# Four sums of a weight quad in another order, and in other tiles

## Chip, core and metric

The kernel runs on one core of a Trainium2 chip. The metric is the time of one execution on the device in microseconds (us); lower is better.

## What is computed

One layer of a hybrid decoder on a sequence of 2048 rows of 1024 values, with 16 learned meta rows ahead of it, all in fp32:

```python
hn = rms_norm(h, norm_g)
proj = jnp.einsum('bld,de->ble', hn, w_in)              # 1024 -> 8 x 512
cx, cb, cc, cg, q, k, v, rg = jnp.split(proj, N_PROJ, axis=-1)
conv_out = short_conv_branch(cx, cb, cc, conv_w) * jax.nn.silu(cg)
qf, kf = rotary(q) * d**-0.5, rotary(k)                 # 4 heads of 128
ret = head_group_norm(retention_chunkwise(qf, kf, v), ret_norm_g)
mixed = jnp.concatenate([conv_out, ret * jax.nn.silu(rg)], axis=-1)
h = h + jnp.einsum('ble,ed->bld', mixed, w_out)
out = rms_norm(h, final_g)[:, N_META:]
```

## The kernel before

The work is two projections, in and out, and between them a short convolution and a chunked retention. TensorE multiplies fp32 values that are split into two parts: a high part, which ScalarE rounds (`wh` for weights, `mh` for the other operand, line 119 or 122), and a low part, the value minus the high part, which VectorE subtracts (`wl`, `ml`, line 120 or 123). A product is then three matmuls for each step of 128: low by high, high by low, high by high.

Most of the projections run as quads: 2 x 2 blocks of weights times 2 x 2 blocks of the other operand, in seven products and not eight (Strassen's scheme in Winograd's form). For that the four weight blocks A11, A12, A21, A22, each 128 x 512, are turned into seven operands: A11, A12, S2, S1, S3, S4, A22 in the order in which `quad` multiplies them, with S1 = A21 + A22, S2 = S1 - A11, S3 = A11 - A21, S4 = A12 - S2. `stationary` makes them: the four sums (helpers `add`, line 128, and `sub`, line 131), and of each operand its two parts. The sums run on GpSimd (POOL); in the very first quad (head 0 of the first half) they run on VectorE (DVE). There are 36 quads in all: 29 on the projection in, 7 on the projection out. The other operand's sums are made ahead of time and are not touched here.

The tiles `ra` are a ring of eight (`RAW`): the four blocks of a quad are loaded into four of them by the SP queue, and `sa`, one more tile of the same ring, holds the one sum that is not written over a block. A block may be overwritten only once its own two parts have been made, and in the first half, where the blocks also feed the meta rows' product (`meta_products`, line 500), once TensorE has read it. The parts `wh` and `wl` have a ring of three each (`RING`), so the parts of a weight operand can be made at most three products ahead.

What is issued in which order on an engine is settled when the program is built: the tile framework runs a simulated clock over the instructions (`schedule_with_timeline_sim=True`) and each engine then executes its own list in order. The kernel adds edges by hand (`tc.issue_after`). Two of them hang on `stationary`: `third[0]` is the low part of S2, behind which the first convolution group is completed (`complete`: four products on VectorE, line 578, then the copies of line 556 and 557 on GpSimd), and `fifth[0]` is the low part of S3, behind which the second pair of output rows adds its first result (`output`, line 128 on `yo`).

The stages in order of time: the start (until about 61 us), in which the x operand of the first half is split, with plain products (lines 303 and 327); the quads of the first half (heads, lines 862 to 902, and convolution groups, lines 556 to 689); from about 361 us the second half; from about 697 us the projection out. There each pair of 128-row blocks is a quad: `take` adds what TensorE gives to the rows of x (line 961 on VectorE, with a first addition of line 128 on GpSimd from the second pair on; of the second pair itself on VectorE), GpSimd multiplies by the final gain (`z`, line 972) and makes the reciprocal roots (`rf`, line 342), and VectorE scales the rows (line 996).

Of the kernel before, what the change touches and what calls it, by code (L numbers as in the profile page):

```python
# [8 lines left out]
F32 = mybir.dt.float32  # L9
# [6 lines left out]
P = 128  # L16
# [6 lines left out]
HB = 512  # L23
# [5 lines left out]
RING, RAW, GEN, COPIES = 3, 8, 16, 4  # L29
# [49 lines left out]
def hybrid_trunk(ctx: ExitStack, tc: tile.TileContext, t, out: bass.AP, chunk_decay):  # L79
# [11 lines left out]
    sb = ctx.enter_context(tc.tile_pool(name="sb", bufs=2))  # L91
# [24 lines left out]
    def split(hi, lo, src, scale=None, eng=nc.vector):  # L116

        if scale is None:
            nc.scalar.copy(out=hi, in_=src)  # L119
            lowered[0] = eng.tensor_tensor(out=lo, in0=src, in1=hi.bitcast(F32), op=ALU.subtract)  # L120
            return
        scaled[0] = nc.scalar.mul(hi, src, scale)  # L122
        nc.vector.scalar_tensor_tensor(  # L123
            out=lo, in0=src, scalar=scale, in1=hi.bitcast(F32), op0=ALU.mult, op1=ALU.subtract
        )

    def add(eng, out, a, b):
        eng.tensor_tensor(out=out, in0=a, in1=b, op=ALU.add)  # L128

    def sub(eng, out, a, b):  # L130
        eng.tensor_tensor(out=out, in0=a, in1=b, op=ALU.subtract)  # L131
# [9 lines left out]
    def stationary(blocks, eng=nc.gpsimd):  # L141

        a11, a12, a21, a22 = blocks
        s1 = sb.tile([P, HB], F32, name="sa", tag="ra", bufs=RAW)

        def parts(src):
            hi = sb.tile([P, HB], F32R, name="wh", tag="wh", bufs=RING)
            lo = sb.tile([P, HB], F32R, name="wl", tag="wl", bufs=RING)
            split(hi, lo, src)
            return hi, lo  # L150

        w = [parts(a11), parts(a12)]
        add(eng, s1, a21, a22)
        sub(eng, a21, a11, a21)
        sub(eng, a11, s1, a11)
        sub(eng, a12, a12, a11)
        w.append(parts(a11))
        third[0] = lowered[0]
        w += [parts(a) for a in (s1, a21)]
        fifth[0] = lowered[0]  # L160
        return w + [parts(a) for a in (a12, a22)]

# [470 lines left out]
    def conv_group(g, r, m, f, blocks, ahead, steps=(), last=False):  # L633
# [27 lines left out]

        blocks, meta = blocks
        quad(stationary(blocks), m, take, behind(0, finish_late, idle, idle))
        catch_up(0)
        if meta:
# [23 lines left out]

        n = 2 * (NG + g) + 1  # L690
        quad(stationary(load_raw(w_loads(n))), m, take, behind(1, idle, gated, idle))
        blocks = ahead()
        def store():
# [55 lines left out]
    def head(h, r, m, rot_t, f, turning, blocks, ahead, sums, first=(), between=((), idle, idle, idle)):  # L749
# [26 lines left out]
        if len(first) > 0:  # L776
            quad_plain(first[0], m, take)
        else:
            with tc.issue_after(spreading[0].ins) if r + h == 0 else nullcontext():
                w = stationary(blocks[0], nc.vector if r + h == 0 else nc.gpsimd)  # L780
            quad(w, m, take, between[0] or (finish_late,))
            catch_up(0)
# [256 lines left out]
    for r in range(NR):  # L1039
# [7 lines left out]
        if r == 0:  # L1047
            w = [[None] * 4 for _ in range(2)]
# [156 lines left out]
```

## Time and profile before

| | |
|---|---|
| median of 3 runs | 867.38 us (866.9 to 867.75) |
| the profiled execution | 867.37 us; its span, first to last instruction, 865.6 us |
| TensorE (PE) busy | 854.3 us, 99% of the span, 4216 matmuls |
| VectorE (DVE) busy | 719.0 us, 83% |
| ScalarE (ACT) busy | 499.1 us, 58% |
| GpSimd (POOL) busy | 373.2 us, 43% |
| granted TensorE clock | 0.997 of full speed |

Busy is the time in which an engine executed something; waits are not in it. In the views below a row names the line of the kernel, the engine, the operation and its tiles as `out<-in`, with shapes as partitions x elements. In a row of an engine's order in time stand the start and the duration in us, and, in brackets, the idle time of the engine ahead of it and what ended it.

### The profile page before, as it was taken

The page shows a single profiled execution, that of the slowest core. Times are in us where ns is not written, and L with a number is a line of the kernel's source. Part 1 is how long each engine was busy: PE and PEld are TensorE (multiplying, and loading weights), DVE is VectorE, ACT ScalarE, POOL GpSimd, SP SyncE. Part 2 cuts the span into 40 slices and gives each one's busy share as a digit, 9 for nine tenths or more (in the row PEclk, how much of TensorE's full clock was granted, in tenths as well). Part 3 has the DMA queues.
Part 4 walks back from the last instruction along what each step waited for, and adds up shares of the span by engine and source line. Part 5 has one row for each costly group of instructions (what it writes and reads, how often), then busy time and mean ns, then how long its engine had stood idle before and what let it go on. Part 6 is the DMA issues. An engine that isn't in the chain of part 4 may idle for free.

```text
span 865.6 us, 12697 instructions
## 1 busy us (share of the span) xinstructions
PE 854.3 (99%) x4216; PEld 705.0 (81%) x4216; DVE 719.0 (83%) x1204; ACT 499.1 (58%) x901; POOL 373.2 (43%) x278
## 2 busy tenths in 40 slices
PE   9999999999999999999999999999999999999996
PEld 6778888878887778788888888888888888788885
DVE  7788989888897977989789898988767799877663
ACT  8775648474855554948374757544433566545553
POOL 0023232423245554352242323354746555678773
PEclk9999999999999999999999999999999999999998
DMA  9714245454656633845263746646122484545431
GB/s 326 252 62 98 61 97 161 112 146 135 158 173 192 195 98 98 320 142 147 62 158 122 164 129 127 202 114 216 49 77 82 175 324 136 168 164 185 151 135 73
DMA packets 127506, 129.51 MB, mean 150 GB/s; under 512 B 58384, under 2 KB 76112, under 8 KB 127440
## 3 DMA queue, kind: packets, MB, share of 16 engines
q1 hardware_dynamic: 126864, 128.30, 49.7%
q8 instruction: 33, 0.54, 0.3%
q10 hardware_dynamic: 576, 0.40, 0.1%
q14 instruction: 33, 0.27, 0.1%
HBM read 90.91 MB, written 25.17 MB: 134 GB/s over the span
## 4 chain that ended last, share of the span: by engine, by line
PE 86%; DVE 6%; issue 2%; ACT 0%; POOL 0%; POOLq 0%; DVEq 0%
PE pj L246 73%; PE pj L303 5%; PE ms L886 2%; PE ms L875 2%; PE ms L885 2%; PE ms L862 2%; DVE wl L120 1%; PE ms L500 1%; DVE ml L120 1%; DVE yo L128 0%; DVE ml L123 0%; DVE yo L961 0%; PE pj L327 0%; DVE yo L996 0%; ACT n L442 0%
## 5 line engine op out<-in xcount | busy, mean ns | idle before, releaser
L246 PE MATMUL pj<-mh,wl 128*128 128x512 f32 x1008 | 395.9, 393 | 1.6 <-DVE wl L120 1.1
L246 PE MATMUL pj<-mh,wh 128*128 128x512 f32 x1008 | 393.2, 390 | 0.0
L246 PE MATMUL pj<-ml,wh 128*128 128x512 f32 x1008 | 392.7, 390 | 0.0
L119 ACT CAST wh<-ra 128x512 fp32r<-128x512 f32 x216 | 134.0, 620 | 232.5 <-PE pj L246 193.3
L120 DVE TENSOR_TENSOR wl<-ra,wh 128x512 fp32r<-128x512 f32 x216 | 192.4, 893 | 40.8 <-ACT wh L119 39.9
L246 PEld LDWEIGHTS pj<-mh,wl 128*128 128x128 f32 x1008 | 189.3, 188 | 43.1 <-issue 2.3
L246 PEld LDWEIGHTS pj<-mh,wh 128*128 128x128 f32 x1008 | 189.3, 188 | 39.5
L246 PEld LDWEIGHTS pj<-ml,wh 128*128 128x128 f32 x1008 | 189.3, 188 | 38.1
L131 POOL TENSOR_TENSOR ra<-ra 128x512 f32<-128x512 f32 x70 | 115.1, 1644 | 101.6 <-PE ms L500 51.3
L128 POOL TENSOR_TENSOR sa<-ra 128x512 f32<-128x512 f32 x35 | 52.7, 1505 | 102.3 <-DVE wl L120 39.8
L131 POOL TENSOR_TENSOR ra<-sa,ra 128x512 f32<-128x512 f32 x35 | 49.9, 1425 | 81.3 <-DVE wl L120 74.1
L253 ACT COPY tc<-pj 128x512 f32<-128x512 f32 x108 | 62.6, 580 | 0.1
L898 POOL TENSOR_TENSOR rp<-rs,neg_half 128x4 f32<-128x4 f32 x16 | 18.9, 1183 | 45.0 <-DVE rs L128 44.9
L961 DVE TENSOR_TENSOR yo<-pj,yo 128x512 f32<-128x512 f32 (+1 forms) x33 | 22.0, 671 | 16.2 <-PE pj L246 8.1
L972 POOL TENSOR_TENSOR z<-yo,final_g 128x512 f32<-128x512 f32 x16 | 26.8, 1674 | 18.6 <-DVE yo L961 18.6
L647 POOL TENSOR_TENSOR c<-c,rr 128x512 f32<-128x512 f32 x14 | 25.0, 1789 | 21.1 <-DVE c L688 11.1
L119 ACT CAST wh<-sa 128x512 fp32r<-128x512 f32 x36 | 22.2, 618 | 17.4 <-PE pj L246 17.1
L647 POOL TENSOR_TENSOR c<-c,tc 128x512 f32<-128x512 f32 x14 | 23.2, 1659 | 19.9 <-ACT tc L673 19.7
L128 DVE TENSOR_TENSOR tc<-pj,tc 128x512 f32<-128x512 f32 x28 | 19.2, 684 | 13.5 <-PE pj L246 13.3
L902 DVE TENSOR_SCALAR pm<-ms,mv,rp 128x128 f32<-128x128 f32 x64 | 21.8, 402 | 10.2 <-POOL rp L898 10.2
L123 DVE SCALAR_TENSOR_TENSOR ml<-x,gain,mh 128x512 fp32r<-128x512 f32 x32 | 25.2, 822 | 5.5 <-ACT mh L122 5.4
L120 DVE TENSOR_TENSOR wl<-sa,wh 128x512 fp32r<-128x512 f32 x36 | 28.9, 804 | 0.8 <-ACT wh L119 0.7
(161 smaller groups left out, 1256.0 us busy)
## 6 DMA issues: line engine op xcount, KB each, us to landing
ra<-in_w_in SPq DMA_DIRECT2D x124, 256.0 KB, 2.8
x<-in_xT SPq DMA_DIRECT2D x48, 256.0 KB, 4.9
w<-in_w_out SPq DMA_DIRECT2D x32, 256.0 KB, 4.5
ra<-mixed SPq DMA_DIRECT2D x32, 256.0 KB, 2.7
yo<-in_x SPq DMA_DIRECT2D x32, 256.0 KB, 4.9
ra<-in_x SPq DMA_DIRECT2D x16, 256.0 KB, 3.4
mixed<-c SPq DMA_DIRECT2D x16, 256.0 KB, 2.4
sums_x<-x SPq DMA_DIRECT2D x16, 256.0 KB, 2.8
```

The costliest lines, as they stand in the source:

```text
L119: nc.scalar.copy(out=hi, in_=src)
L120: lowered[0] = eng.tensor_tensor(out=lo, in0=src, in1=hi.bitcast(F32), op=ALU.subtract)
L123: nc.vector.scalar_tensor_tensor(out=lo, in0=src, scalar=scale, in1=hi.bitcast(F32), op0=ALU.mult, op1=ALU.subtract)
L128: eng.tensor_tensor(out=out, in0=a, in1=b, op=ALU.add)
L131: eng.tensor_tensor(out=out, in0=a, in1=b, op=ALU.subtract)
L246: nc.tensor.matmul(bank, a[:, ks], b, start=first and kt == 0 and n == 0, stop=kt == KH - 1 and n == 2, skip_group_check=not first,)
L253: copied[0] = nc.scalar.copy(out=c, in_=bank)
L303: nc.tensor.matmul(banks[i], a[:, ks], b, start=half + kt + n == 0, stop=half == 1 and kt == KH - 1 and n == 2,)
L647: eng.tensor_tensor(out=out, in0=a, in1=b, op=ALU.mult)
L902: nc.vector.tensor_scalar(out=y[:, cs], in0=o[:, cs], scalar1=mv[:, c, 0:1], scalar2=rp[:, c, :], op0=ALU.subtract, op1=ALU.mult,)
L961: last[0] = nc.vector.tensor_tensor(out=y[:, cs], in0=pp[:, cs], in1=y[:, cs], op=ALU.add)
L972: nc.gpsimd.tensor_tensor(out=ys[i][j], in0=y, in1=final_g[:, j * HB : (j + 1) * HB], op=ALU.mult)
```

## The change

The four sums are made in the order S1, S2, S3, S4. S1 is written over A21. S2 is S1 - A11, over A11 as before. S3 is now A22 - S2, which is A11 - A21 again, and lies in the tile `sa`; it needs S2, and A21 no longer. S4 is as before. The order in which the seven operands are split and multiplied stays.

```diff
-        s1 = sb.tile([P, HB], F32, name="sa", tag="ra", bufs=RAW)
+        s3 = sb.tile([P, HB], F32, name="sa", tag="ra", bufs=RAW)
...
         w = [parts(a11), parts(a12)]
-        add(eng, s1, a21, a22)
-        sub(eng, a21, a11, a21)
-        sub(eng, a11, s1, a11)
+        add(eng, a21, a21, a22)
+        sub(eng, a11, a21, a11)
+        sub(eng, s3, a22, a11)
         sub(eng, a12, a12, a11)
         w.append(parts(a11))
         third[0] = lowered[0]
-        w += [parts(a) for a in (s1, a21)]
+        w += [parts(a) for a in (a21, s3)]
         fifth[0] = lowered[0]
         return w + [parts(a) for a in (a12, a22)]
```

## The prediction

> **What bounds the kernel now.** I read the page first (span and busy shares), then the order in time of TensorE to find every place where it loses a step, then the groups of the three kinds of sum, and last the order in time of VectorE and GpSimd around those places.
>
> ```profile
> span 865.6 us, 12697 instructions
> ...
> PE 854.3 (99%) x4216; PEld 705.0 (81%) x4216; DVE 719.0 (83%) x1204; ACT 499.1 (58%) x901; POOL 373.2 (43%) x278
> ```
>
> TensorE is busy for 854.3 of 865.6 us, so no edit beside it can bring more than the few microseconds in which it stands still. The next rows are TensorE's own, in time; the last bracket is idle time and what ended it.
>
> ```profile
> 60.13 0.39 PE L246 MATMUL pj<-ml,wh 128*128 128x512 f32 x1
> 60.36 0.39 PE L246 MATMUL pj<-mh,wh 128*128 128x512 f32 x1
> 61.22 0.47 PE L246 MATMUL pj<-mh,wl 128*128 128x512 f32 x1 [0.47 <-DVE wl L120]
> ...
> 295.72 0.39 PE L246 MATMUL pj<-mh,wh 128*128 128x512 f32 x1
> 296.74 0.47 PE L246 MATMUL pj<-mh,wl 128*128 128x512 f32 x1 [0.63 <-DVE wl L120]
> ...
> 360.00 0.39 PE L303 MATMUL pj<-mh,mh 128*128 128x512 f32 x1
> 361.40 0.50 PE L303 MATMUL pj<-mh,ml 128*128 128x512 f32 x1 [1.01 <-DVE ml L120]
> ...
> 740.34 0.39 PE L246 MATMUL pj<-mh,wh 128*128 128x512 f32 x1
> 741.24 0.50 PE L246 MATMUL pj<-mh,wl 128*128 128x512 f32 x1 [0.51 <-DVE yo L961]
> ```
>
> The step from one matmul to the next is 60.36 - 60.13 = 0.23 us (they overlap). Against it four places lose over half a microsecond each: A at 61.22, 0.86 - 0.23 = 0.63; B at 296.74, 0.79; C at 361.40, 1.17; E at 741.24, 0.67. Together 3.26 us, or 0.38% of the span: that is the whole stake. All four are ended by VectorE. So the question is not when GpSimd has S2, but what VectorE does just ahead of these four matmuls.
>
> Now the sums themselves (columns: count, busy, mean ns, idle of the engine before them and what ended it):
>
> ```profile
> L131 POOL TENSOR_TENSOR ra<-ra 128x512 f32<-128x512 f32 x70 | 115.1, 1644 | 101.6 <-PE ms L500 51.3
> L128 POOL TENSOR_TENSOR sa<-ra 128x512 f32<-128x512 f32 x35 | 52.7, 1505 | 102.3 <-DVE wl L120 39.8
> L131 POOL TENSOR_TENSOR ra<-sa,ra 128x512 f32<-128x512 f32 x35 | 49.9, 1425 | 81.3 <-DVE wl L120 74.1
> ```
>
> The 35 in the middle are S1, the 35 below are S2, the 70 above are S3 and S4. S2 waited 81.3 us in all, 74.1 of them for a `wl`: that is the low part of A11, which must have been read before S2 may overwrite A11. It did not wait for S3, which GpSimd had made long before.
>
> **The change part by part.**
>
> *Removed and added instructions.* None: four sums a quad before and after, on the same engine, 128x512 each. On GpSimd the order S1, S3, S2, S4 becomes S1, S2, S3, S4. No DMA is issued more or less. A wait for a free fifth tile goes from S1 (39.8 us of its idle time) to S3, and S3 gets a new input, S2.
>
> *S2 a place earlier on GpSimd.* Nothing, where S2 waits for the `wl` of A11 (the 74.1 us): S1 is still made while GpSimd idles, S2 starts at the same instant, and only S3 moves, from ahead of that wait to behind S2. In the four quads of the first half that also feed the meta products, S3 waits for TensorE to have read A21 (51.3 us in the row of 70); there S1 now writes A21 and inherits the wait. S2 is again the second sum behind it. Zero, with the S2 as early as before.
>
> *What S3's move does to VectorE.* This is where time can come from. Over the whole trace one form of VectorE's subtraction, both inputs in SBUF, took:
>
> ```profile
> L120 DVE TENSOR_TENSOR wl<-sa,wh x36: 672/680/1792, 63.4 to 843.6; 128x512 fp32r<-128x512 f32 x36
> ```
>
> 680 ns in the median and 1792 at most (minimum, median, maximum). The long ones lie under a sum on GpSimd, so a GpSimd sum costs VectorE up to 1.79 - 0.68 = 1.11 us where VectorE is in a hurry. The Trainium skill (SBUF — State Buffer, Who interferes with whom) says that a VectorE instruction with two SBUF inputs and a GpSimd instruction that reads SBUF exclude each other for the whole instruction; by that rule an unlucky start would cost the full sum, an estimate of 1.4 to 1.6 us instead of 1.11, and the sum below would still come out the same, since the gap it closes is smaller than either. So S3's place matters only at A, B, C and E.
>
> *E, the second pair of output rows.*
>
> ```profile
> 732.10 1.73 POOL L128 TENSOR_TENSOR sa<-ra 128x512 f32<-128x512 f32 x1 [0.94 <-DVE wl L120]
> 733.91 1.62 POOL L131 TENSOR_TENSOR ra<-ra 128x512 f32<-128x512 f32 x1
> ...
> 734.31 1.77 DVE L128 TENSOR_TENSOR yo<-yo,tc 128x512 f32<-128x512 f32 x1
> ...
> 740.49 0.69 DVE L961 TENSOR_TENSOR yo<-pj,yo 128x512 f32<-128x512 f32 x1
> ...
> 742.90 1.74 POOL L131 TENSOR_TENSOR ra<-sa,ra 128x512 f32<-128x512 f32 x1
> ```
>
> The addition at 734.31 took 1.77 instead of 0.68 us, under the S3 of the next quad (733.91). The addition at 740.49, which gives the bank back to TensorE, stands behind it in VectorE's order. After the change that S3 comes behind its S2 (742.90), over 9 us later, and the chain to 740.49 is up to 1.77 - 0.68 = 1.09 us shorter. The gap holds 0.67, so all of it goes. Ends: -0.67, and 0 if S1, no longer held by its tile, lands in the same VectorE chain a second time's worth. I take -0.67, since S1 only moves within the chain and S3 leaves it. Late next would be TensorE itself.
>
> *B.* There the S3 of the following quad leaves the VectorE chain too, but the quad's own S3 (before, ahead of the chain) enters it behind S2. One out, one in, at 1.11 each: 0, with ends -0.79 (the gap) and +1.11.
>
> *C, where the second half's first operands are made.*
>
> ```profile
> 342.29 1.29 POOL L131 TENSOR_TENSOR ra<-sa,ra 128x512 f32<-128x512 f32 x1 [0.48 <-DVE rc L413]
> ...
> 344.74 0.68 DVE L120 TENSOR_TENSOR wl<-ra,wh 128x512 fp32r<-128x512 f32 x1
> ```
>
> And from the chain that ended last:
>
> ```profile
> 345.55 1.62 POOL ra L131
> 347.17 1.51 POOL u L647
> ...
> 360.67 0.69 DVE ml L120
> ```
>
> S2 ends at 343.58. S3 now follows, 343.6 to about 345.2 at the 1.62 of a disturbed sum. The `wl` of A12 at 344.74 lies under it: it ends near 345.8 instead of 345.42, and S4 (345.55, which waits for it) starts about 0.4 later. S4 is on the chain: `u` behind it on GpSimd, then the taps, then the `ml` at 360.67 that TensorE waits for. Bounds: 0, if S3 is done by 344.74, and +1.62, a whole sum. I take +0.4, nearest to the overlap that the rows give.
>
> *A, the first quad, whose sums are VectorE's.*
>
> ```profile
> 54.22 0.68 DVE L128 TENSOR_TENSOR sa<-ra 128x512 f32<-128x512 f32 x1
> 55.58 0.68 DVE L131 TENSOR_TENSOR ra<-ra 128x512 f32<-128x512 f32 x1
> 57.38 0.68 DVE L131 TENSOR_TENSOR ra<-sa,ra 128x512 f32<-128x512 f32 x1
> ...
> 58.09 0.62 ACT L119 CAST wh<-ra 128x512 fp32r<-128x512 f32 x1 [0.91 <-DVE ra L131]
> ...
> 59.19 0.68 DVE L131 TENSOR_TENSOR ra<-ra 128x512 f32<-128x512 f32 x1
> ...
> 60.39 0.68 DVE L120 TENSOR_TENSOR wl<-ra,wh 128x512 fp32r<-128x512 f32 x1
> ```
>
> Here S1, S3, S2, S4 are VectorE's, and the third product waits for S2's low part at 60.39. S2 moves from 57.38 to 55.58, 1.8 us earlier, and its cast with it. But the cast was done at 58.71, and VectorE still made S4 (59.19) before the low part (60.39): by the code all four sums stand ahead of it. With S3 where S2 was, four sums are still ahead, and 60.39 stays. Ends: -0.63, all of the gap, if the low part overtakes S4 (one step of VectorE, 0.6, does it), and +1.11, if the second quad's S1, no longer held for its tile, falls on GpSimd under this chain. I take 0, the row order as it stands.
>
> *All other quads.* S3 falls between S2 and S4, and S4 comes later by at most a sum, 1.6 us. TensorE has S4 as its sixth product, 3 products or 36 x 0.23 = 8 us behind S2's: nothing. That cover goes only where GpSimd's queue behind S4 holds something urgent; that is the second rival.
>
> Sum: A 0, B 0, C +0.4, E -0.67, together -0.3. The profiled execution took 867.37 (its span 865.6 and 1.8 around it), the median of the three runs is 867.38, so no correction: 867.1 us.
>
> **The rivals.**
>
> *First: the low part of S2 overtakes S4, and the chains at B and E lose a GpSimd sum.* -0.63 - 0.79 - 0.67 = -2.1, without a loss at C: 865.3. For it: the stated order of the sums puts S2 exactly where A waits, and all three chains are VectorE's with sums under them. Against it: at A the rows show S4 ahead of a low part that was ready. The least gain that counts, 1.73 us (0.2%, about what a measurement of this kernel can tell from no change), needs three of the four gaps.
>
> *Second, on the other side: in the output loop S3 holds up the reciprocal roots.*
>
> ```profile
> 761.64 1.74 POOL L131 TENSOR_TENSOR ra<-sa,ra 128x512 f32<-128x512 f32 x1
> 763.46 1.29 POOL L131 TENSOR_TENSOR ra<-ra 128x512 f32<-128x512 f32 x1
> 764.71 0.55 POOL L342 TENSOR_TENSOR rf<-rs_v,neg_half 128x1 f32<-128x1 f32 x1
> ...
> 769.46 0.68 DVE L120 TENSOR_TENSOR wl<-sa,wh 128x512 fp32r<-128x512 f32 x1
> ...
> 771.29 0.39 PE L246 MATMUL pj<-mh,wl 128*128 128x512 f32 x1
> ...
> 843.63 1.79 DVE L120 TENSOR_TENSOR wl<-sa,wh 128x512 fp32r<-128x512 f32 x1
> ...
> 847.45 0.39 PE L246 MATMUL pj<-mh,wl 128*128 128x512 f32 x1
> ```
>
> S2, S4 and `rf` run without a break. With S3 between them `rf` comes up to 1.74 us later, the scaling of the rows behind it, then the low part for the fourth product (769.46 to 770.14), which has 1.15 us to spare before 771.29. It would be 0.59 late. In the last pair 847.45 - 845.42 = 2.03 is to spare, and nothing is lost; over the six steady pairs that falls, carried back in a line, from some 0.7 to 0, about 2 us: 869.1 to 869.4. It decides from a delay of `rf` over 1.15 us on. Against it: S3 has left the stretch ahead of S2 where GpSimd also works without a break, so S2 itself may come up to 1.7 us earlier and pay for it.
>
> *Third: the change does not do what it says.* S2 is no earlier on TensorE's clock anywhere, S3 only moves about: 867.4 within 0.5. This is my forecast without its two small terms, and gives the same verdict.
>
> **How the numbers follow.** Forecast with its near relative (third): 0.69. First rival: 0.17. Second, or a sum of GpSimd landing in the chains at A, B or C (+1.1 to +1.6 each): 0.14. These are the chances of same, faster and slower. The range goes from 865.3, the first rival's value, to 868.9, which takes in one landing of +1.6 but not the whole of the second rival: it leaves out some 0.18. The forecast alone would be 866.0 to 868.0.
>
> **What would show it.** The wait at 741 gone and the one at 361 longer by some tenths; the row of S1 without its wait for `wl`, that row of idle time now at S3; S2's 74 us of waiting for `wl` unchanged; the low part of the first quad's S2 still behind S4. Wrong would be: a low part ahead of S4 at 60 us; new TensorE waits in the output loop; loads of the next quad that take the tile before S3 does, so that S3 waits for its own quad's third split.

## The result, and the profile after

| | before | after |
|---|---|---|
| median of 6 runs, us | 867.37 (866.38 to 867.75) | 873.62 (873.18 to 874.89) |
| profiled execution, its span | 867.37, 865.6 | 873.5, 871.7 |
| granted TensorE clock | 0.997 | 0.999 |

The changed kernel is slower by 6.25 us: ratio 1.0076, 95% interval 1.0066 to 1.0086. The prediction was 867.1, and its range ended at 868.9. The clock is no cause.

The page of the changed kernel, span and busy shares:

```profile
span 871.7 us, 12664 instructions
...
PE 857.9 (98%) x4216; PEld 704.5 (81%) x4216; DVE 717.6 (82%) x1204; ACT 499.1 (57%) x901; POOL 370.4 (42%) x278
```

Of the engines beside TensorE none is busy for longer: VectorE 717.6 us (719.0 before), GpSimd 370.4 (373.2). TensorE runs the same 4216 matmuls. So the sums do not stop VectorE for longer in all; they stop it at other places. The groups of the three kinds of sum (columns as in the prediction):

```profile
L131 POOL TENSOR_TENSOR ra<-ra 128x512 f32<-128x512 f32 x70 | 106.4, 1520 | 110.3 <-issue 79.1
L128 POOL TENSOR_TENSOR ra<-ra 128x512 f32<-128x512 f32 x35 | 54.2, 1549 | 160.7 <-DMA ra<-in_w_in 77.9
...
L131 POOL TENSOR_TENSOR sa<-ra 128x512 f32<-128x512 f32 x35 | 52.6, 1504 | 2.3
```

The 70 are now S2 and S4, the 35 in `sa` are S3. S1 (middle row) no longer waits for a `wl` but most of all for its load. S3 hardly ever waits: 2.3 us in 35. It stands right behind S2 every time. Whether S2 still waits 74 us for the `wl` of A11 can't be read from its row: of its 110.3 us of idle time, 79.1 stand as `issue`, time for which the profile shows no releaser. What TensorE waited for (us in all, times, longest):

```profile
PE pj L303 <- DVE ml L120: 2.4, 2, 1.4
PE pj L246 <- DVE wl L120: 1.8, 4, 0.5
...
PE ms L885 <- DVE pm L877: 0.8, 2, 0.4
```

The third row is new; the first was 1 wait before, and the second was 2. TensorE's own rows at C, in a head of the second half, and at E:

```profile
363.52 0.50 PE L303 MATMUL pj<-mh,ml 128*128 128x512 f32 x1 [1.37 <-DVE ml L120]
...
514.13 0.49 PE L885 MATMUL ms<-v,pm 128*128 128x128 f32 x2 [0.40 <-DVE pm L877]
...
747.12 0.39 PE L246 MATMUL pj<-mh,wh 128*128 128x512 f32 x1
747.35 0.39 PE L246 MATMUL pj<-mh,wl 128*128 128x512 f32 x1
```

C waits 1.37 instead of 1.01; E's wait is gone (step 0.23). The rest of the loss lies where there was no wait before. To find it I set the n-th of the 3408 projection matmuls (lines 246, 303, 327) of each trace against the n-th before, and took how much the difference of their starts grows over each stretch of before's time. This is worked out from the traces, one execution of each kernel, in us; + is lost. The last column is the difference of the spans, which is not quite that of the medians (order_only: 2.74 here, 2.02 there):

| kernel | 0–67 | 67–104 | 104–269 | 269–357 | C: 357–362 | 425–581 | 581–656 | 656–742 | all |
|---|---|---|---|---|---|---|---|---|---|
| after | 0.14 | 0.65 | 0.06 | 0.77 | 0.50 | 1.72 | 1.17 | 0.99 | 6.15 |
| order_only | 0.10 | 0 | -0.09 | -0.36 | 0.51 | 1.56 | 0.05 | 0.51 | 2.74 |
| tiles_only | 0.27 | 0 | 1.73 | -0.09 | 0 | -0.02 | 0.04 | 0.25 | 2.44 |
| own_ring | 0.95 | 0.64 | 0.03 | 1.59 | 0.48 | 1.26 | 0.88 | 0.80 | 6.96 |
| s1_free | -0.94 | 0 | -0.09 | -0.25 | 0.49 | 1.21 | 0.25 | 0.57 | 1.24 |
| s1_free_old | 0.14 | 0 | 0.05 | -0.72 | 0.01 | 0 | 0.02 | 0.44 | 0.02 |
| s1_behind | 0.36 | 0.65 | 0.05 | 0.73 | 0.51 | 1.98 | 0.97 | 0.97 | 6.21 |
| out_only | 0.06 | 0 | 0.04 | -0.76 | -0.65 | 0 | 0.04 | 0.13 | -0.96 |
| first_and_out | -1.10 | 0 | 0.05 | -0.71 | -0.01 | 0.01 | 0.04 | 0.27 | -1.46 |
| no_s3 | 0.72 | 0 | -0.09 | -0.45 | -0.01 | -0.02 | -0.27 | -0.25 | -0.36 |
| late_memset | -0.03 | 0 | -0.09 | -0.89 | 0 | -0.02 | -0.27 | -0.13 | -1.27 |

The stretch 362–425 and the output loop behind 742 (0.5 or less) are left out, but for s3_twice, told below. `out_only` has the engines' lists of before until about 700 us; its -0.76 and -0.65 (the wait at B is gone and that at C shorter, without any change ahead of them) are what one execution differs from another there. So differences under 0.8 us between 269 and 362 us say nothing by themselves. From 425 to 581 us it shows 0, and there a tenth counts.

Three stretches with a clear loss, beside C, can be followed to a cause: the heads of the second half (425 to 581), the convolution quads (581 to 656), and one place at 104 us. The head at 452 us, first before, then after, VectorE and GpSimd in order of time, and TensorE's first matmul with `pm`:

```profile
450.07 1.29 POOL L131 TENSOR_TENSOR ra<-sa,ra 128x512 f32<-128x512 f32 x1 [7.56 <-DVE wl L120]
...
451.94 0.69 DVE L709 TENSOR_TENSOR rot<-qg,rot_t 64x512 f32<-64x512 f32 x1
452.05 1.73 POOL L131 TENSOR_TENSOR ra<-ra 128x512 f32<-128x512 f32 x1 [0.68 <-POOL ra L131]
452.65 1.67 DVE L710 TENSOR_TENSOR rot<-qg,rot_t 64x512 f32<-64x512 f32 x1
...
464.77 0.68 DVE L877 SCALAR_TENSOR_TENSOR pm<-ms,causal 128x512 f32<-128x512 f32 x1
466.05 0.38 PE L885 MATMUL ms<-v,pm 128*128 128x128 f32 x2
```

```profile
452.18 1.30 POOL L131 TENSOR_TENSOR ra<-ra 128x512 f32<-128x512 f32 x1 [8.91 <-issue]
453.56 1.61 POOL L131 TENSOR_TENSOR sa<-ra 128x512 f32<-128x512 f32 x1
454.06 1.66 DVE L709 TENSOR_TENSOR rot<-qg,rot_t 64x512 f32<-64x512 f32 x1
455.13 1.75 POOL L131 TENSOR_TENSOR ra<-ra 128x512 f32<-128x512 f32 x1
455.73 1.70 DVE L710 TENSOR_TENSOR rot<-qg,rot_t 64x512 f32<-64x512 f32 x1
...
467.62 0.68 DVE L877 SCALAR_TENSOR_TENSOR pm<-ms,causal 128x512 f32<-128x512 f32 x1
468.36 0.49 PE L885 MATMUL ms<-v,pm 128*128 128x128 f32 x2
```

S2 comes 452.18 - 450.07 = 2.11 us later, which is what had been lost by then; against TensorE it did not move. Before, the first rotation of the head's query (line 709) started 0.11 ahead of S4, with GpSimd idle until then, and ran in 0.69; the second (710) was stopped by S4. After, S3 fills that pause, and both are stopped. The masked scores (`pm`, line 877), which TensorE multiplies next, come 467.62 - 464.77 = 2.85 later, 0.74 more than the 2.11. Before, `pm` was ready at 465.45, 0.60 ahead of the matmul at 466.05: less room than that. The next head, at 514 us, shows TensorE waiting 0.40 for `pm`. Three heads of this stretch lose, TensorE's steps there grow by 0.30, 0.67 and 0.71; with the rest of the stretch that is 1.72 us.

### The profile page after: what moved, and what is told of

Its sections match the earlier page's. It is cut to its first block, busy times and chain, and to the rows that moved or that the text cites. A ratio compares the mean times of both kernels' runs of the same rounds, so it can differ in the third digit from the quotient of the medians.

```text
span 871.7 us, 12664 instructions
## 1 busy us (share of the span) xinstructions
PE 857.9 (98%) x4216; PEld 704.5 (81%) x4216; DVE 717.6 (82%) x1204; ACT 499.1 (57%) x901; POOL 370.4 (42%) x278
## 4 chain that ended last, share of the span: by engine, by line
PE 49%; DVE 11%; ACT 4%; issue 3%; DMA 1%; POOL 1%; SPq 0%; POOLq 0%; DVEq 0%; ACTq 0%
PE pj L246 42%; PE pj L303 4%; DVE wl L120 3%; DVE ml L120 1%; ACT wh L119 1%; DVE w L131 1%; PE ms L885 1%; DMA ra<-in_w_in 1%; PE ms L886 1%; DVE rot L709 1%; PE ms L875 1%; DVE rot L710 1%; DMA w<-in_w_out 1%; ACT kd L814 1%; DVE qg L915 0%
## 5 line engine op out<-in xcount | busy, mean ns | idle before, releaser
L131 POOL TENSOR_TENSOR ra<-ra 128x512 f32<-128x512 f32 x70 | 106.4, 1520 | 110.3 <-issue 79.1
L128 POOL TENSOR_TENSOR ra<-ra 128x512 f32<-128x512 f32 x35 | 54.2, 1549 | 160.7 <-DMA ra<-in_w_in 77.9
L120 DVE TENSOR_TENSOR wl<-sa,wh 128x512 fp32r<-128x512 f32 x36 | 26.7, 742 | 10.0 <-ACT wh L119 9.9
L565 DVE SCALAR_TENSOR_TENSOR c<-u,conv_w,c 128x512 f32<-128x512 f32 x32 | 30.0, 973 | 1.8 <-ACT c L563 1.3
L128 DVE TENSOR_TENSOR tc<-pj,tc 128x512 f32<-128x512 f32 x28 | 19.1, 684 | 14.8 <-PE pj L246 14.7
```

Source lines behind the costliest of these rows:

```text
L565: nc.vector.scalar_tensor_tensor(out=c, in0=u[:, tap : tap + HB], scalar=conv_w[:, g, tap : tap + 1], in1=c, op0=ALU.mult, op1=ALU.add)
```

## Experiments

The theory: a sum on GpSimd stops VectorE's two-input operations, and what matters is which of them each sum meets; the late S3 meets the heads' rotations, and S1, made over A21, meets others. The first rival: the tiles; S3 in the fifth tile holds it longer, the loads come late and in bunches (the `ra` loads of the SP queue, which before came in ones and twos between 437 and 448 us, came three together at 432 us). The second rival: any extra work on GpSimd between S2 and S4 does it, since S4 and what stands behind it come late.

**order_only.** The order of the change, the tiles of before.

```diff
-        sub(eng, a21, a11, a21)
         sub(eng, a11, s1, a11)
+        sub(eng, a21, a22, a11)
```

> The order of the change with the tiles of before: S1 stays in the fifth tile, and S3 = A22 - S2 is written over A21 behind S2. Theory 1: a GpSimd sum stops VectorE for about 1.1 us where both inputs of VectorE lie in SBUF, and S3's late place puts one sum more into stretches in which VectorE is behind; then this kernel has nearly all of the loss, 872 to 874 us, with the new TensorE waits at the heads of the second half (matmuls of line 885). Theory 2: S3's tile, taken late from the ring of eight, holds back the loads behind it (three at once behind a transpose, where they stood singly before); here the fifth tile is taken by S1, early, as before, so the time is that of before, 867.4 within 0.8.

869.65 us (869.32 to 870.66; before, run beside it, 867.63), ratio 1.0026 (1.0016 to 1.0035): about a third of the loss, between the two forecasts. The order alone costs, but it is not nearly all. It has the heads' 1.56 and C's 0.51, and next to nothing at 104 and at 581 to 656 us. The head again:

```profile
451.63 3.31 POOL L131 TENSOR_TENSOR ra<-ra 128x512 f32<-128x512 f32 x2
452.12 1.66 DVE L709 TENSOR_TENSOR rot<-qg,rot_t 64x512 f32<-64x512 f32 x1
453.80 1.69 DVE L710 TENSOR_TENSOR rot<-qg,rot_t 64x512 f32<-64x512 f32 x1
```

The same two stopped rotations, without any change of tiles.

**tiles_only.** The tiles of the change; since S1 then overwrites A21, S3 has to come first.

```diff
-        add(eng, s1, a21, a22)
-        sub(eng, a21, a11, a21)
-        sub(eng, a11, s1, a11)
+        sub(eng, s1, a11, a21)
+        add(eng, a21, a21, a22)
+        sub(eng, a11, a21, a11)
...
-        w += [parts(a) for a in (s1, a21)]
+        w += [parts(a) for a in (a21, s1)]
```

> The tiles of the change with S3 early: S3 = A11 - A21 first, into the fifth tile, then S1 over A21, S2, S4. Theory 1: S3 is out of the late stretches, 867.4 within 0.8. Theory 2 says nothing sharp here, since the fifth tile is taken early again. Theory 3, that S1 over A21 is what costs (it waits until TensorE has read A21 in the four quads with meta products): 869 or more, with the loss before 300 us.

870.84 us (869.84 to 871.13), ratio 1.0032 (1.002 to 1.0045). That is the number of theory 3, and theory 1 missed. It loses at none of the change's places, but 1.73 us between 104 and 269:

```profile
105.31 1.67 POOL L131 TENSOR_TENSOR sa<-ra 128x512 f32<-128x512 f32 x1 [3.84 <-DVE wl L120]
105.95 3.28 DVE L578 TENSOR_TENSOR c<-c,cb 128x512 f32<-128x512 f32 x2
107.06 1.63 POOL L128 TENSOR_TENSOR ra<-ra 128x512 f32<-128x512 f32 x1
```

Two sums in a row lie under two multiplications that took 1.28 together before (105.67). What follows on VectorE comes later by that, and TensorE waits 0.60 for a `kv` at 120.89; a wait of 0.38 for a `wl` at 176.77 is most of the rest. S1 does not wait here for TensorE's reading of A21, as theory 3 had it: it follows S3, which waited for a `wl`. It is the same mechanism at another place.

**no_s3.** S3 is not computed; the fifth product takes A21 as loaded. **s3_twice.** S3 as before and once more, behind S2.

```diff
-        sub(eng, a21, a11, a21)                          # no_s3
...
-        sub(eng, a11, s1, a11)                           # s3_twice
+        sub(eng, a11, s1, a11); sub(eng, a21, a22, a11)
```

> The kernel before with the subtraction that makes S3 left out: the fifth product gets A21 as it was loaded, so 36 instructions of about 1.5 us are missing. Theory 1: nothing late, and the sum that stood under the addition of the second output pair is gone too: 866.7, the wait at 741 us gone, and the gap between this kernel and the one with the late order is what S3's late place costs. If GpSimd's time as such counted, it would be far lower, 864 or less.

> The kernel before with one sum more: S3 early as before, and made again as A22 - S2 over the same tile behind S2. So the late sum is added to the early one and nothing is moved. If the late place is what costs, the heads of the second half lose at least the 1.6 us of the run with the order alone, and the whole is 869.5 or more. If the order alone lost by what S3 no longer did early, or by the tile's later use, this stays near 868.

no_s3: 865.57 us (864.76 to 867.0), ratio 0.9973 (0.9961 to 0.9985), between the forecast 866.7 and the 864 that would have spoken for GpSimd's time as such. s3_twice: 884.89 (884.79 to 885.11; before 867.08), ratio 1.0203 (1.0188 to 1.0218): the late place costs, far more than the 869.5 named, and the heads (425 to 581 us) lose 2.99. The busy shares of no_s3, then of s3_twice:

```profile
PE 854.6 (99%) x4216; PEld 705.6 (82%) x4216; DVE 677.2 (78%) x1203; ACT 499.6 (58%) x901; POOL 313.9 (36%) x243
```

```profile
PE 860.2 (97%) x4216; PEld 703.8 (80%) x4216; DVE 752.7 (85%) x1205; ACT 497.4 (56%) x901; POOL 426.3 (48%) x313
```

Taking S3 out of its early place gives VectorE 719.0 - 677.2 = 41.8 us back; one of the 36 was VectorE's own (0.68), so 41.1 / 35 = 1.17 us for each sum. Of this only 867.63 - 865.57 = 2.06 us reached the time, 0.06 a quad: the early place is nearly free. A second S3 at the late place adds 33.7 to VectorE (0.94 a sum, reckoned alike), and 17.8 to the time, 0.49 a quad; 3.7 of it are in the output loop, 0.62 for each of six pairs. That is the price of one more sum on top of the early one, not of moving it; moving it cost 2.0 (order_only).

**late_memset.** S3 is not computed; in its late place GpSimd fills A21's tile twice with a constant, behind S2.

```diff
-        sub(eng, a21, a11, a21)
-        sub(eng, a11, s1, a11)
+        s2 = eng.tensor_tensor(out=a11, in0=s1, in1=a11, op=ALU.subtract)
+        with tc.issue_after(s2.ins): [eng.memset(a21, v) for v in (0.5, 0.25)]
```

> As the run with the order alone, but behind S2 two memsets of A21 stand in place of the subtraction (S3's value is left out): GpSimd is kept busy at the same place and reads nothing. If GpSimd and VectorE shut each other out through reads of SBUF, the rotations behind S2 in the heads of the second half run in their usual 0.69 us and the 1.6 us that the order alone lost there between 425 and 581 us are gone: 867 or less. If it is the time on GpSimd or the place in its list that counts, the loss there stays: 869 to 870.

866.54 us (865.85 to 867.03; before 867.08), ratio 0.9992 (0.9982 to 1.0001), as forecast for a stop that comes of reads. The group of the memsets, the head and the busy shares:

```profile
L155 POOL MEMSET ra<- 128x512 f32 x70 | 36.8, 525 | 1.1
```

```profile
450.29 0.53 POOL L155 MEMSET ra<- 128x512 f32 x1
450.92 0.69 DVE L709 TENSOR_TENSOR rot<-qg,rot_t 64x512 f32<-64x512 f32 x1
451.03 1.72 POOL L131 TENSOR_TENSOR ra<-ra 128x512 f32<-128x512 f32 x1 [0.21 <-POOL ra L155]
```

```profile
PE 853.7 (99%) x4216; PEld 705.3 (82%) x4216; DVE 680.2 (79%) x1205; ACT 499.5 (58%) x901; POOL 341.1 (39%) x313
```

36.8 us of extra work on GpSimd in the late place, and VectorE is busy 680.2, as good as without S3 at all (677.2). The memsets did meet VectorE: by the rows, 19.1 of the 36.8 us lay over operations with two inputs in SBUF, and the six such operations that had a memset and nothing else of GpSimd over them took 0.68 to 0.69 each. The heads lose nothing (-0.02), with the first rotation at 0.69. In the head shown one memset stood ahead of S4 and one behind it, and they are shorter than a sum (0.53 against 1.6), so this is not the whole delay of S4; but it rules out that GpSimd's being busy is enough. The second rival falls as far as these 0.53 us go.

**own_ring.** The change, with S3 in a tile of its own and one tile less in the ring.

```diff
-RING, RAW, GEN, COPIES = 3, 8, 16, 4
+RING, RAW, GEN, COPIES = 3, 7, 16, 4
...
-        s3 = sb.tile([P, HB], F32, name="sa", tag="ra", bufs=RAW)
+        s3 = sb.tile([P, HB], F32, name="sa", tag="s3", bufs=1)
```

> The changed kernel, with S3 in a tile of its own and the ring of the blocks at seven (the same memory). Loads no longer stand behind S3's tile. If the hold on the loads costs (theory 2), the 3.5 us by which the change is slower than the order alone go in large part: 870 to 871. If it is S1 over A21, which may start as soon as its blocks are there, and S3 behind S2 (theory 1), they stay: 872.5 or more, with the waits at 104 us, at 603 to 658 us and before 704 us.

873.86 us (872.55 to 874.86; before 867.08), ratio 1.0074 (1.0059 to 1.0089): the whole loss, in the same stretches, as theory 1 had it. S3's hold on the ring is not the cause; the first rival falls.

**out_only.** The whole change in the seven quads of the projection out alone (`stationary` takes a flag that only those set).

> Order and tiles of the change in the seven quads of the projection out alone. Theory 1: the next pair's S3 leaves the chain to the addition at 740.49, the wait of 0.67 us there goes as it did in the changed kernel, and VectorE has time to spare in the later pairs: 866.7, between 866.3 and 867.1. Theory 2: the loads of the pairs come later and TensorE waits in the output loop: 868 or more.

867.27 us (866.33 to 869.02; before 867.63), ratio 0.9997 (0.9988 to 1.0006): a little above the forecast 866.3 to 867.1. The wait at 741 us is gone, but no difference can be told in the whole. In the output loop the change costs nothing.

**s1_free, s1_free_old.** What the tiles add to the order is more than what the order costs (6.25 - 2.02 = 4.2). In these two S1 lies in a tile of its own and not over A21; s1_free has the order of the change, s1_free_old that of before.

```diff
-RING, RAW, GEN, COPIES = 3, 8, 16, 4
+RING, RAW, GEN, COPIES = 3, 7, 16, 4
...
-        s1 = sb.tile([P, HB], F32, name="sa", tag="ra", bufs=RAW)
+        s1 = sb.tile([P, HB], F32, name="sa", tag="s1", bufs=1)
```

> The order alone (S1, S2, S3, S4, S3 over A21) with S1 in a tile of its own, so that S1 neither waits for a tile of the ring nor, as it does in the changed kernel, for TensorE to have read A21. The order alone took 869.65 us, the whole change 873.6. Theory one (S1 set free falls under VectorE's chains in the convolution quads; S1 over A21 falls into the chain at 104 us only because it waits for the meta products): the stretch from 581 to 656 us loses 0.8 to 1.2 us against before, where the order alone lost 0.05; the stretch up to 104 us loses nothing; the heads of the second half lose their 1.5 us as with the order alone; total 870.5 to 871.5. Rival (what the tiles cost is S3's, in the fifth tile, not S1's freedom): 581 to 656 us stays at 0.05, total 869.6. Rival two (a free S1 is simply earlier and gains): under 869.

> The order of before (S1, S3, S2, S4) with S1 in a tile of its own. Theory one: S1 and S3 together come earlier where the fifth tile held them back, and lie under other VectorE operations; the heads of the second half lose nothing (S3 is not behind S2), the convolution quads at 581 to 656 us lose up to 1.2 us; total 867.5 to 868.6. If S1's freedom costs nothing: 867.4 within 0.5. If it is of use (sums done before VectorE's chains begin): 866.5 or less.

s1_free: 868.78 us (868.18 to 870.5; before 867.34), ratio 1.002 (1.001 to 1.0029). s1_free_old: 867.39 (865.41 to 867.67), ratio 0.9993 (0.9983 to 1.0003). The expectation for s1_free missed at 581 to 656 us: 0.25, not 0.8 to 1.2. Its total is that of rival two (under 869), but a gain by a freer S1 is not shown: s1_free_old has none, and the interval of its ratio overlaps with that of order_only. A ring of one does not set S1 free: its row there is

```profile
613.04 1.74 POOL L647 TENSOR_TENSOR c<-c,rr 128x512 f32<-128x512 f32 x1 [1.64 <-DVE c L565]
615.41 1.29 POOL L128 TENSOR_TENSOR sa<-ra 128x512 f32<-128x512 f32 x1 [0.63 <-DVE wl L120]
```

It still waits for the low part of the S1 before it, and so stays behind `c<-c,rr`. What the pair shows: with S1 off A21, the losses at 104 us (0) and most of those at 581 to 656 us go, in either order, and the heads' (1.21) stay with the late S3. So the tile that costs is S1's. It costs there only together with the late order: tiles_only, with S1 over A21 too and S3 early, loses 0 and 0.04 at the two places. The same place in the changed kernel:

```profile
615.04 3.11 DVE L565 SCALAR_TENSOR_TENSOR c<-u,conv_w,c 128x512 f32<-128x512 f32 x3 [0.32 <-ACT c L563]
616.10 1.51 POOL L128 TENSOR_TENSOR ra<-ra 128x512 f32<-128x512 f32 x1 [1.20 <-DMA ra<-in_w_in]
617.56 1.74 POOL L647 TENSOR_TENSOR c<-c,rr 128x512 f32<-128x512 f32 x1
618.08 1.77 DVE L120 TENSOR_TENSOR wl<-ra,wh 128x512 fp32r<-128x512 f32 x1
...
619.40 0.39 PE L246 MATMUL pj<-mh,wh 128*128 128x512 f32 x1
619.90 0.50 PE L246 MATMUL pj<-mh,wl 128*128 128x512 f32 x1
```

A21 itself is never split, so an S1 over it needs only its load: it starts ahead of `c<-c,rr` and lies over VectorE's products of line 565. The three take 3.11, where they take 2.08 in s1_free (611.54), so the `wl` behind them starts 1.03 later against them. That `wl` is stopped by `c<-c,rr` in both (1.77 and, at 613.54, 1.79). In the changed kernel it comes too late, and the step from 619.40 to 619.90 is 0.50 instead of 0.23. And the place at 104 us, before and then after:

```profile
96.27 1.52 POOL L131 TENSOR_TENSOR ra<-ra 128x512 f32<-128x512 f32 x1 [13.46 <-PE ms L500]
...
101.66 1.28 DVE L578 TENSOR_TENSOR c<-c,rr 128x512 f32<-128x512 f32 x2
103.06 0.68 DVE L120 TENSOR_TENSOR wl<-ra,wh 128x512 fp32r<-128x512 f32 x1
```

```profile
96.35 1.59 POOL L128 TENSOR_TENSOR ra<-ra 128x512 f32<-128x512 f32 x1 [19.72 <-PE ms L500]
...
101.32 1.72 POOL L131 TENSOR_TENSOR ra<-ra 128x512 f32<-128x512 f32 x1
101.83 2.36 DVE L578 TENSOR_TENSOR c<-c,rr 128x512 f32<-128x512 f32 x2
...
104.31 0.68 DVE L120 TENSOR_TENSOR wl<-ra,wh 128x512 fp32r<-128x512 f32 x1
```

Before, S1 had been made at 81.5 us and three sums stood behind TensorE's reading of the blocks (line 500); now all four do, the last one lies over `c<-c,rr` (2.36 for two instead of 1.28), and the `wl` behind it is 1.25 later.

**s1_behind.** The whole change, but in the second half's convolution quads and behind them S1 is issued behind `c<-c,rr` of the group before.

```diff
...
-        add(eng, a21, a21, a22)
+        with tc.issue_after(gate_mul[0].ins) if gate_mul[0] else nullcontext(): add(eng, a21, a21, a22)
...
-            mul(nc.gpsimd, cs[j], cs[j], rr[j])
+            made = nc.gpsimd.tensor_tensor(out=cs[j], in0=cs[j], in1=rr[j], op=ALU.mult); gate_mul[0] = made if r == j == 1 else gate_mul[0]
```

> The whole change, but in the second half's convolution quads and behind them S1 is issued on GpSimd behind the first multiplication by the gate factor (`c<-c,rr`) of the group before, and so no longer ahead of it. TensorE's, ScalarE's lists are those of the changed kernel. Theory one (S1 over A21, held by nothing but its load, goes ahead of that multiplication, which then lies under VectorE's `wl`): the fourth products that waited at 619.9 and 658.4 us in the changed kernel no longer wait; the stretch from 581 to 656 us loses 0.3 to 0.5 us against before, where the whole change lost 1.17; total 872.8 to 873.1. Rival (the stretch loses by the late S3 there, or by the loads): it still loses 1.0 to 1.2 us, total 873.6.

873.48 us (873.28 to 875.59; before 867.01), ratio 1.0077 (1.0064 to 1.0091): no gain. Both forecasts were half right. At the two places the wait went:

```profile
616.13 2.08 DVE L565 SCALAR_TENSOR_TENSOR c<-u,conv_w,c 128x512 f32<-128x512 f32 x3 [0.31 <-ACT c L563]
618.13 1.79 DVE L120 TENSOR_TENSOR wl<-ra,wh 128x512 fp32r<-128x512 f32 x1
```

The products of line 565 are back at 2.08, the step of the fourth product is 0.23 again (620.48 to 620.71), and against the changed kernel some 0.4 us come back at each of the two places. But the S1 of the quad before now stands behind a `c<-c,rr` at 590.69 us, and S2, `c<-c,tc`, S3 and S4 come behind it, without a pause, from 592.51 on. They lie over VectorE's preparation of the output weights (`w`, 2.88 for the two at 593.51) and a `wl` (1.78 at 596.31), for which TensorE waits 0.37 at 598.24. Between 581 and 600 us 0.94 is lost, against 0.31 in the changed kernel. The stretch as a whole: 0.97. Sums that leave one chain land in the next.

**first_and_out.** The order of the change in the very first quad and the seven of the projection out, that of before elsewhere; S1 in a tile of its own. It takes the stretches in which s1_free gained.

```diff
...
-        sub(eng, a21, a11, a21)
-        sub(eng, a11, s1, a11)
+        late or sub(eng, a21, a11, a21)
+        sub(eng, a11, s1, a11); late and sub(eng, a21, a22, a11)
```

> The order of before in all quads but the very first and the seven of the projection out, which have the order S1, S2, S3, S4; S1 in a tile of its own. Theory one: the gap at 61 us goes, since all four of the first quad's sums are done earlier in this variant (0.6 to 0.9 us), the heads of the second half and the copies at 361 us lose nothing, and the wait at 741 us goes (0.3 to 0.7 us): 866.0 to 866.6, a fifth of a per cent below before at the most. Rival (the sums of the first quad in this order gain only together with those of the second, or the output loop's ends are spread over run-to-run differences): 867.4 within 0.4.

866.47 us (865.25 to 868.04; before 867.01), ratio 0.9995 (0.9987 to 1.0004): no difference that can be told, though the waits at A and E are gone, that at A as in s1_free (there the low part starts at 58.87 and its matmul at 60.55, against 61.22 before).

## Why the prediction was wrong

*A* was right: the low part (60.53) stayed behind S4 (58.73), and the wait stayed: 0.46 at 61.36, 0.47 before. *B* still waits (0.54 at 298.01); more can't be told apart from the spread between executions there. *E* was right in sign, size and cause: the wait at 741 us is gone, and the addition that S3 stopped takes 0.69:

```profile
740.05 0.69 DVE L128 TENSOR_TENSOR yo<-yo,tc 128x512 f32<-128x512 f32 x1
```

The wait alone would not show it: tiles_only lacks it too, with the addition still at 1.77 (736.13), since TensorE comes later there. And S1 has left the chain as well, where the prediction had it move only within it. *C* was right in sign and size, +0.4 against 0.50 measured. One execution alone could not show it, but the five kernels of the table in which S3 only comes late have 0.48 to 0.51, and tiles_only, s1_free_old, first_and_out, no_s3 and late_memset 0.01 at most, so it is the late S3 that does it. That S4 is the link was not shown: the chain that ended last reaches that `ml` through ScalarE's rounding ahead of it. The loads did not take S3's tile, and the output loop (second rival) lost nothing. S2's place on TensorE's clock did not change, as forecast.

The step that failed is the sentence "So S3's place matters only at A, B, C and E", with "All other quads ... nothing". It was reached by looking only for places where TensorE already waited, and by taking the 8 us until S4's product as the cover. The price of a sum was near: 1.11 at most was said, and no_s3 gives 1.17 in the mean, a little more than the most. The 1.4 to 1.6 us that the prediction estimated for an unlucky start does not show on one operation: the longest `wl` before took 1.85 (774.87), 1.17 over the usual 0.68. But the sum does not delay S4's product; it delays whatever VectorE does meanwhile, and in the heads that is a chain with next to no room: rotations, states, `pm`, TensorE. The room of a weight's low part was checked, the room of `pm` was not: it was 0.60 at the head shown. That is 1.72 us in the changed kernel, 1.56 with the order alone, and 1.21 to 1.98 in the other three kernels with the late S3. The prediction's own row carried the warning: the 101.6 and 81.3 us of idle GpSimd said that sums can move freely, not that what lies beside them can bear it.

The second failed step is "there S1 now writes A21 and inherits the wait. S2 is again the second sum behind it. Zero". S2 was indeed as early, but four sums and not three now stand behind the wait: 0.65 us at 104 us. The third is the wait that "goes from S1 ... to S3": treated as bookkeeping. S1's wait for the fifth tile had been holding it behind `c<-c,rr`; without it, and with the late S3, the convolution quads lost 1.17. The third rival ("only moves about") named the right mechanism and gave it no price.

Open: 656 to 742 us loses 0.99, after E gave back 0.67. The largest part is where the projection out begins: at 703.70 TensorE waits 1.00 for an `ml`, where it did not wait before. The trace leads some way: the multiplication `u<-u,tc`, which GpSimd makes behind S4, starts 4.94 us behind S2 (684.71 to 689.65) where it was 4.28, and lies over the first product of line 565 (1.58 instead of 0.74); the next, `c<-c,rr`, lies over a `wl` (1.78 instead of 0.68); from there to that `ml` VectorE has no long pause. s1_free has both (1.58 and 1.79), and its matmul there comes 1.12 later, 1.16 in the changed kernel. But in no_s3, late_memset and first_and_out, without a late S3 there, it comes some 0.36 later too, so the share of the late S3 is not shown. Between 269 and 357 us the changed kernel stands at +0.77, kernels of before's order between -0.89 and 0, and order_only and s1_free at -0.36 and -0.25; what the change does there is not shown. Nor is it shown how the 4.2 us of the tiles split between those stretches.

## What to carry to other kernels

When an operation moves on an engine that shares something with another, list what the other engine does at the new place, and follow each of these to the next wait of the bounding engine; a wait that is 0 today may be 0 by half a us (0.60 here). A wait for a buffer can be what keeps work out of a busy stretch: before taking it away, ask where the work will run then. Equal busy totals (719.0 and 717.6 us of VectorE) can differ by 6 us of time.

## What the runs showed of the hardware

GpSimd's writes alone do not stop VectorE: 70 memsets of 0.525 us in the late place left VectorE's busy time at 680.2 us, against 677.2 without them, while 35 sums, in their early place, made it 719.0. Nor is a VectorE operation stopped that takes one of its two inputs from PSUM (`pj`), before at 507 us:

```profile
507.01 1.62 POOL L131 TENSOR_TENSOR ra<-ra 128x512 f32<-128x512 f32 x1
507.40 0.68 DVE L128 TENSOR_TENSOR kv<-pj,tc 128x512 f32<-128x512 f32 x1
```

In the trace of before 53 operations of that kind lay under a sum for 0.3 us or more, and none took over 0.70. The Trainium skill (SBUF — State Buffer, Who interferes with whom) says both: two SBUF inputs on VectorE contend with a GpSimd instruction that reads SBUF, not with one that only writes, and with one SBUF input, outside VectorE's two-port modes, there is no contention. These traces agree: 0.68 to 0.69 us under a memset, at most 0.70 with an input from PSUM under a sum, up to 1.85 for a `wl` with two inputs in SBUF (774.87, before). It works the other way too: where VectorE runs operations with two inputs in SBUF without a break, a GpSimd multiplication took 5.25 us by the profile (changed kernel, at the end of the last convolution group), against 1.30 for the same one of an earlier group of order_only (668.73):

```profile
701.37 5.25 POOL L647 TENSOR_TENSOR c<-c,tc 128x512 f32<-128x512 f32 x1 [6.09 <-ACT tc L673]
```

It ends 1.24 us behind the start of VectorE's next operation with an input from PSUM (`tc<-pj,tc`, 705.38), about the 1.30 that it takes alone. In before, order_only, tiles_only, s1_free and own_ring the same multiplication takes 4.31 to 5.15 us and ends 1.23 to 1.24 us behind the start of that addition. So GpSimd seems to get in only there: this is inferred from the times, no run here moved that addition.
